# The low part of k in the second block's attention: one tile of two halves, or two zero-padded tiles

## The chip, the cores and the metric

The kernel runs on one core of one Trainium2 chip. The metric is the device time of one execution in microseconds (us). One launch computes two transformer blocks over 1,024 tokens of 1,024 features. The three runs shown below lie within 0.1% of each other.

## The reference, cut to what matters

The change lies in the second block's attention: 24 heads of 64 features in three groups of eight. In each group a query sees a causal window of its own residue class (dilation 1, 4 or 16), worked in blocks of 128 queries against the block itself and the one before it.

```python
HEAD_DIM = 64
HEADS_PER_GROUP = 8
DILATION_GROUPS = ((128, 1), (512, 4), (2048, 16))
...
    scores = jnp.einsum('bdhnqe,bdhnke->bdhnqk', qb.astype(jnp.float32),
                        kb.astype(jnp.float32)) * (e ** -0.5)
...
    scores = jnp.where(mask, scores, NEG_INF)
    m = jnp.max(scores, axis=-1)
    p = jnp.exp(scores - m[..., None])
    den = jnp.sum(p, axis=-1)
    o = jnp.einsum('bdhnqk,bdhnke->bdhnqe', p, vb.astype(jnp.float32)) / den[..., None]
```

## The kernel before, in words

**Precision.** TensorE multiplies in a reduced form of float32, so each operand is split into a hi and a lo part whose sum is exact; a product is hi·hi + hi·lo + lo·hi. Heads have only 64 features, so for the scores two of the three terms share one product over 128 partitions. `stack_q` makes, per head, a tile `qs` with hi on one half of the partitions and lo on the other; `stack_k` makes a tile `ks` with the hi part of k on both halves (the second half by a DMA of the first). The product of the two gives hi·hi + lo·hi. The third term, q's hi times k's lo, is a second product into the same place in PSUM; the lo parts of the two heads stand in the two halves of one tile `kl`, so this product contracts over 64 partitions, 0 to 63 for the first head of a pair and 64 to 127 for the second.

**Staging.** `block2` runs 12 pairs of heads (4 pairs hp in each of 3 groups g). A pair (`att_pair`) is: products q, k and v (`in2`, 48 matmuls of 512 columns each, whose weight tile is loaded as `w`, cast by ScalarE to `w2h` and subtracted by VectorE or GpSimd to `w2l`); rope; the stacks; transposes of v (`vt`); then for each head the scores (`as`: a `ks` and a `kl` product for each of 8 query blocks), the row maximum (`ap`, `amx`, VectorE), the exponentials (`ap`, ScalarE), transposes of those (`apt`), their split (`apth`, `aptl`) and the products with v (`ao`). Gate tiles (`z_conv`, `z_att`, `g_att`, `FILL`) follow each pair as filler for TensorE, and the taps of a convolution (`conv`) run on VectorE and GpSimd as background work. The masks, the exponentials and the sums are the same for every pair; a block has 256 key columns in the groups of dilation 1 and 4 (128 where it has no predecessor) and 128 in that of dilation 16.

**What sets the order.** The kernel records its instructions on virtual tiles, and a list scheduler in the kernel fixes one order per engine at build time: among the ready instructions it takes the one that is earliest in the program, up to 3,000 instructions ahead (`win`; 450 for SP, which issues the loads). Most tiles come from one pool of 50 pages of 128 x 1,024 float32 (`PAGES`). An instruction that writes a new tile takes a page when it is ordered, and it may do so early only if the count of live pages stays at 50 or under on the way to its own place in the program (`allowed`). On the chip it then waits until the page's last user is done.

Of the kernel before, what the change touches and what calls it, by code (L numbers as in the profile page):

```python
# [20 lines left out]
# ------------------------------------------------------------------ deferred program  # L21
# The kernel records its instructions on virtual tiles first; a list scheduler then fixes one
# order per engine (ready instructions by program order) and the instructions are issued to Tile
# in that order.
# [28 lines left out]
class VT:  # L53
    """A virtual tile: a slot of a pool from its first instruction to its last."""
# [13 lines left out]
class V:  # L68
    """A view of a virtual tile, resolved when its instruction is issued."""
# [24 lines left out]
    def region(self):  # L94
        """Bounds in the tile of what the view touches (at least)."""
        r = [(0, n) for n in self.t.shape]
        dims = list(range(len(r)))  # axes of the tile that the view still has
        if self.t.kind == "pb":  # a matmul that opens a group concerns its whole bank
            return tuple(r)
# [60 lines left out]
class Rec:  # L160
    """Records the calls on one engine."""
# [27 lines left out]
class Program:  # L189
    # margin of an operand that comes from another engine (us)  # L190
    LAT = 0.5

    def __init__(self, tc, nc, pools, limits):
        self.tc, self.nc, self.pools, self.limits = tc, nc, pools, limits
        self.engines = {"pe": nc.tensor, "act": nc.scalar, "dve": nc.vector, "pool": nc.gpsimd, "sp": nc.sync}
        self.ops, self.vts = [], []
        self.pe, self.act, self.dve, self.pool, self.sp = (Rec(self, e) for e in ("pe", "act", "dve", "pool", "sp"))
        self.count = 0
        self.bias = 0
        self.far = 0  # how far ahead of the oldest unfinished instruction one may be issued  # L200
        self.win = {None: 3000, "sp": 450}

    # -------------------------------------------------------------- tiles
# [6 lines left out]
    def dram(self, ap):  # L210
        """A DRAM scratch array whose order the program keeps."""
        return VT(self, "dram", ap.shape, F32, "dram", real=ap).v()

    # -------------------------------------------------------------- recording
    def record(self, eng, cost, lat, issue, reads, writes):
# [3 lines left out]
        op.dma = 0.0  # time that it takes of the DMA queues  # L219
# [25 lines left out]
    def price(self, eng, fn, a, kw, wr, rd):  # L245
        """Estimated time on the engine (us) and extra latency until the result can be used."""
# [35 lines left out]
    # -------------------------------------------------------------- scheduling  # L282
# [115 lines left out]
# ---------------------------------------------------------------- host layout  # L398
def _tiles(w, cols=None):
    """[K, C] -> [C/128, 128 (k within tile), K/128, 128 (c within tile)]."""  # L400
# [7 lines left out]
def _rows(w):  # L408
    """[K, C] -> [128 (k within tile), K/128, C]."""
# [5 lines left out]
def _vec(v):  # L415
    """[n*128] -> [128, n]."""
    return np.asarray(v).reshape(-1, P).T
# [10 lines left out]
def _selections():  # L428
    """Rows of the transposed trig tile: 16 cos, 8 cos, 16 sin, 8 sin, one."""
# [20 lines left out]
def _fourier_tables():  # L450
# [3 lines left out]
    tab = np.stack([np.cos(th) / 256, -np.sin(th) / 256])  # [2, 256 p, 1024 t = 4m+r]  # L454
    tab = tab.reshape(2, 2, P, 256, 4).transpose(1, 0, 2, 4, 3)  # [half, cs, p, r, m]
# [3 lines left out]
    ch = np.stack([np.concatenate([cc, cc], 1), np.concatenate([ss, ss], 1)], 1)  # [64, 2, 128]  # L459
# [3 lines left out]
def _band_masks():  # L463
    """Masks added to minus the scores: [prev | cur] band, [cur | none], and two causal blocks of 64."""
# [10 lines left out]
def prep(inp):  # L475
# [16 lines left out]
    o["wf"] = np.ascontiguousarray(g["w_fourier"][0].transpose(1, 0, 2))  # [64 c, 8 g, 64 e]  # L492
    o["ftab"], o["fch"] = _fourier_tables()
    o["w_out"] = _tiles(g["w_out"][0])
    o["memT"] = np.ascontiguousarray(g["mem"][0].T.reshape(2, 4, P, 256).transpose(0, 2, 1, 3))  # [2, p, 4 k, m]
# [3 lines left out]
    w = _tiles(g["w_mem_o"][0])  # [8 m, p, 8 k, 128]  # L499
# [30 lines left out]
# first 128-column tile of each part of w_in_2  # L530
# [3 lines left out]
# channel tiles of the convolution that run on ScalarE and GpSimd  # L534
POOL_CONV = (3,)
# steps of the latent attention with one of the memory's keys and values
MEM_AT = range(20,32)
# weight tiles of the experts split ahead of their products
AHEAD = 5
# and loaded ahead of them  # L540
RAW = 38
# of them before the first product
START = 38
# and right behind the first rows of an expert
# [3 lines left out]
# eighths of the work that VectorE and GpSimd can both do that GpSimd takes, by phase  # L548
# [3 lines left out]
# uses of the expert weights that are left when the second block's trig tables are loaded  # L552
TR = 16
# weight tiles of the second block that may be loaded before its input is there
# [3 lines left out]
# heads of the memory's attention by part of the output product  # L558
PARTS = ((0, 1), (2, 3))
# weight tiles of the experts loaded with each tile of these products  # L560
PRE = ((1, 1, 1, 1, 1, 1, 1, 1), (2, 2, 2, 2, 2, 2, 2, 2))
# instructions of the convolution behind each half product of the second block
TICKS = dict(zip("qkvgz", (1, 2, 1, 2, 2)))
# gate tiles behind each pair of heads, and tiles of the convolution ahead of each three pairs
# [4 lines left out]
class Halves:  # L569
    """Two tiles that hold one half each."""  # L570
# [8 lines left out]
class Kern(Program):  # L579
# [57 lines left out]
    # hi / lo halves of a float32 tile (exact: hi + lo == x)  # L637
    def split(self, x, base="sp", shape=(P, NT), hi="act", lo=None, scale=None, kind="pg"):
        """x: float32 AP in SBUF or PSUM; scale: per-partition column multiplied in."""
# [5 lines left out]
    def ve(self):  # L645
        """VectorE or GpSimd, by the share of the phase."""
# [18 lines left out]
    def wtile(self, dram, nk, base="w", hi="act", lo=None):  # L665
        """One stationary weight chunk [128, nk, 128] as hi / lo."""
# [9 lines left out]
    def gemm_t(self, w, xs, evac, n=NT, base="mm", ticks=2):  # L676
        """evac(c, ps): ps[128 cols, tokens c..] = sum_k w[:, k, :]^T xs[k], half of the tokens at a time."""
# [12 lines left out]
    def tick(self, last=None, n=2):  # L690
        """Background work (a vector queue, and one on ScalarE and GpSimd), a few instructions per half product."""
# [8 lines left out]
    def rsqrt(self, out, a, n):  # L700
        """out = a ** -0.5 on a small [128, n] tile (sqrt, reciprocal, one Newton step)."""
# [9 lines left out]
    def rsqrt_dve(self, out, a, n):  # L711
        """The same without a table of ScalarE: a guess from the exponent and three Newton steps."""
# [10 lines left out]
    def touch(self, func, after):  # L723
        """Have the table of an activation function in place once the instructions of after are done."""
# [4 lines left out]
    def colsum(self, tiles, n=8):  # L729
        """Sum over features (partitions of all tiles) -> psum [128 tok, n]: natural token layout."""  # L730
# [7 lines left out]
    def bcast_rows(self, col, evac, n=8):  # L738
        """[128 tok, n] small tile -> evac(tokens, psum): the token vector along the free axis in every partition."""
# [16 lines left out]
    # ------------------------------------------------------------------ trig  # L756
    def trig(self):
        """Transposed trig rows [49, 1024] for both position sets (block 1 freqs use positions, block 2 positions_2)."""
# [12 lines left out]
        # 2 pi = A + B + C with A, B of 12 bits; k = k1 + k0, k1 a multiple of 2048  # L771
# [48 lines left out]
    # ------------------------------------------------------------------ block 1, first half  # L820
    def block1_in(self):
# [3 lines left out]
        # the first weights and tokens come in halves, for an early start  # L825
# [20 lines left out]
        # latents: raw products (row factor deferred) times the gain, and their squares  # L846
# [34 lines left out]
        for name, n in (("q_lat", 3), ("kv_lat", 2)):  # L881
            # rx (rx^2 S / n + eps)^-1/2 = (S / n + eps / rx^2)^-1/2
# [7 lines left out]
        # rope key (rows 64..127, twice)  # L890
# [1137 lines left out]
```

## Time and profile before

| | before |
|---|---|
| device time, median of 3 runs | 2846.16 us (2844.48 to 2846.61) |
| the profiled execution, first to last instruction | 2844.7 us |
| TensorE busy | 2742.3 us, 96% of the span |
| VectorE busy | 2083.7 us, 73% |
| ScalarE busy | 1366.3 us, 48% |
| GpSimd busy | 479.1 us, 17% |
| mean granted TensorE clock | 0.970 of 2.4 GHz |
| second block's attention (first to last score product) | 1602.9 to 2482.1 us |

The profile is of one execution; its span is 1.5 us under the median of the timed runs. TensorE's matmuls are pipelined, so the "busy" time of one matmul is longer than its share of the engine: what a matmul costs is the distance from its start to the start of the next.

### The profile page before, as it was taken

To read this page: it belongs to the slowest core of one execution; us is meant where nothing else is said; L and a number is where in the kernel's file an instruction comes from. 1 tells how busy PE (TensorE), PEld (TensorE's weight loads), DVE (VectorE), ACT (ScalarE), POOL (GpSimd) and SP (SyncE) were. 2 spreads that over 40 slices of the span, in tenths; PEclk is the share of its full clock that TensorE was granted. 3 is DMA by queue.
4 is the path that set the end of the run, shared out by engine and by line. 5 is a ranking of instruction groups with operands and counts; after the bars stand their busy time and mean duration, and the time that the engine had idled before them with its cause. 6 is when DMAs were issued, how large, how long until landed. Compare 5 with 4: busy or idle time off the path is not lost. (4 is left out here: it accounts for less than half of the span.)

```text
span 2844.7 us, 35896 instructions
## 1 busy us (share of the span) xinstructions
PE 2742.3 (96%) x13230; PEld 2271.2 (80%) x13230; DVE 2083.7 (73%) x3075; ACT 1366.3 (48%) x2177; POOL 479.1 (17%) x246
## 2 busy tenths in 40 slices
PE   8999999999996999999979989999999999999998
PEld 6888898888874888888868777877888788887887
DVE  7368876358567899988968888787699886549553
ACT  6157766234345777777852445244233344423221
POOL 1124565111023200000010333201000002001000
PEclk9999999999997999999989998999999899999999
DMA  4000113345267999999942112112112133348941
GB/s 178 25 35 8 36 53 125 143 157 193 96 238 284 347 362 360 357 375 392 391 151 104 32 51 78 56 60 89 64 40 70 64 120 141 141 140 297 343 180 52
DMA packets 130143, 457.06 MB, mean 161 GB/s; under 512 B 15298, under 2 KB 17538, under 8 KB 129968
## 3 DMA queue, kind: packets, MB, share of 16 engines
q1 hardware_dynamic: 125360, 438.00, 41.9%
q0 software_dynamic: 4608, 16.78, 2.3%
q8 instruction: 104, 1.70, 0.2%
q14 instruction: 71, 0.58, 0.1%
HBM read 378.73 MB, written 69.70 MB: 158 GB/s over the span
## 5 line engine op out<-in xcount | busy, mean ns | idle before, releaser
L180 DVE SCALAR_TENSOR_TENSOR conv<-u,convw,conv 128x1023 f32<-128x1023 f32 (+21 forms) x210 | 290.1, 1387 | 2.3
L180 DVE TENSOR_TENSOR w_upl<-w_up,w_uph 128x1024 fp32r<-128x1024 f32 x128 | 149.2, 1220 | 22.5 <-ACT w_uph L180 22.0
L180 DVE TENSOR_TENSOR w_downl<-w_down,w_downh 128x1024 fp32r<-128x1024 f32 x128 | 148.9, 1219 | 13.3 <-ACT w_downh L180 12.7
L180 DVE TENSOR_TENSOR w_gatel<-w_gate,w_gateh 128x1024 fp32r<-128x1024 f32 x123 | 144.0, 1219 | 8.2 <-ACT w_gateh L180 5.7
L180 ACT CAST w_gateh<-w_gate 128x1024 fp32r<-128x1024 f32 x128 | 125.7, 1055 | 5.7 <-issue 3.4
L180 ACT CAST w_downh<-w_down 128x1024 fp32r<-128x1024 f32 x128 | 126.0, 1055 | 1.4 <-PE ea L180 1.4
L180 ACT CAST w2h<-w 128x1024 fp32r<-128x1024 f32 x80 | 83.2, 1048 | 90.5 <-DMA w<-in_w_in_dram 82.9
L180 ACT CAST w_uph<-w_up 128x1024 fp32r<-128x1024 f32 x128 | 125.8, 1055 | 1.4 <-PE ea L180 0.7
L180 POOL TENSOR_TENSOR w2l<-w,w2h 128x1024 fp32r<-128x1024 f32 x16 | 42.9, 2682 | 421.4 <-ACT w2h L180 389.6
L180 POOL TENSOR_TENSOR wl<-w,wh 128x1024 fp32r<-128x1024 f32 (+3 forms) x31 | 56.2, 1814 | 314.1 <-ACT wh L180 285.2
L180 POOL TENSOR_TENSOR conv<-conv,ct 128x1023 f32<-128x1023 f32 (+29 forms) x30 | 80.6, 2688 | 163.7 <-ACT ct L180 163.2
L180 DVE TENSOR_TENSOR w2l<-w,w2h 128x1024 fp32r<-128x1024 f32 x64 | 87.9, 1376 | 25.7 <-ACT w2h L180 25.1
L180 DVE CUSTOM_DVE_ANT_0 ap<-as,mask 128x128 f32<-128x128 f32 (+1 forms) x192 | 59.9, 352 | 62.0 <-PE as L180 56.8
L180 ACT CAST wh<-w 128x1024 fp32r<-128x1024 f32 (+3 forms) x71 | 62.5, 894 | 77.4 <-DMA w<-in_w_convout_dram 28.4
L180 ACT ACTIVATE ap<-ap,amx 128x128 f32<-128x128 f32 (+1 forms) x192 | 85.5, 447 | 26.7 <-DVE amx L180 26.3
L180 DVE TENSOR_TENSOR ptl<-pt,pth 128x512 fp32r<-128x512 f32 x128 | 81.4, 683 | 8.8 <-ACT pth L180 6.9
L180 ACT ACTIVATE p<-p,mx 128x1024 f32<-128x1024 f32 x64 | 73.8, 1155 | 23.5 <-DVE mx L180 17.2
L180 POOL TENSOR_SCALAR p<-p,sum 128x1024 f32<-128x1024 f32 x64 | 74.5, 1170 | 58.8 <-DVE sum L180 50.6
L180 PE MATMUL ea<-w_gatel,hth 128*128 128x512 f32 x256 | 80.1, 394 | 0.7 <-DVE w_gatel L180 0.7
L180 PE MATMUL eb<-w_uph,hth 128*128 128x512 f32 x256 | 80.5, 394 | 0.1
L180 PE MATMUL ea<-w_gateh,hth 128*128 128x512 f32 x256 | 80.6, 395 | 0.0
L180 PE MATMUL eb<-w_upl,hth 128*128 128x512 f32 x256 | 79.5, 392 | 0.7 <-DVE w_upl L180 0.5
(553 smaller groups left out, 8669.9 us busy)
## 6 DMA issues: line engine op xcount, KB each, us to landing
w_gate<-in_w_gate_dram SPq DMA_DIRECT2D x128, 512.0 KB
w_up<-in_w_up_dram SPq DMA_DIRECT2D x128, 512.0 KB
w_down<-in_w_down_dram SPq DMA_DIRECT2D x128, 512.0 KB
w<-in_w_in_dram SPq DMA_DIRECT2D x89, 512.0 KB
wada<-in_w_adaT_dram SPq DMA_DIRECT2D x24, 512.0 KB
convr<-cd SPq DMA_DIRECT2D x16, 512.0 KB
amd<-sg SPq DMA_DIRECT2D x16, 512.0 KB
ks<-ks SPq DMA_DIRECT2D x24, 256.0 KB
```

What stands on the lines that cost most here:

```text
L180: getattr(k.engines[eng], fn)(*[r(x) for x in a], **{n: r(x) for n, x in kw.items()})
```

## The change

`stack_k` makes two `kl` tiles per pair in place of one. Each holds the lo part of its own head on that head's 64 partitions, and zeros, written by a GpSimd memset, on the other 64. The second score product then takes all 128 partitions of `qs` and of `kl`; the zeros meet q's lo part. The count of products, of weight loads, of subtractions and of DMAs is the same; 24 memsets of 64 x 1,024 and 12 pages are new.

```diff
     def stack_k(self, o):
-        x, l = [self.page("ks", F32R) for _ in range(2)], self.page("kl", F32R)
+        x, l = ([self.page('ks', F32R) for _ in range(2)], [self.page('kl', F32R) for _ in range(2)])
         a, b = slice(0, 64), slice(64, P)
         for i, (own, far) in enumerate(((a, b), (b, a))):
+            self.pool.memset(l[i][far].bitcast(F32), 0.0)
             self.act.copy(x[i][own], o[own])
             self.sp.dma_start(x[i][far].bitcast(F32), x[i][own].bitcast(F32))
-            self.dve.tensor_tensor(l[own], o[own], x[i][own].bitcast(F32), OP.subtract)
+            self.dve.tensor_tensor(l[i][own], o[own], x[i][own].bitcast(F32), OP.subtract)
         return x, l
...
                     op = self.pe.matmul(sb, qs[h][:, q], kst[h][:, kk], start=True, stop=False)
...
-                    self.pe.matmul(sb, qs[h][r, q], kl[r, kk], start=False, stop=True)
+                    self.pe.matmul(sb, qs[h][:, q], kl[h][:, kk], start=False, stop=True)
```

The rest of the change removes comments. A memset depends on nothing but its page, so the scheduler orders it up to 3,000 instructions ahead of its place. GpSimd's order in the last experts of the first block (`hg` is the gather of an expert's rows, `x<-ey` the scatter-add of its result) was:

```order
L1392 DMA hg_11024<-hrow_84,idx 128x1024
L1401 DMA x_4_85<-ey_11107,idx 1024x1024
L1392 DMA hg_11353<-hrow_84,idx 128x1024
L1401 DMA x_4_85<-ey_11463,idx 1024x1024
L1392 DMA hg_11704<-hrow_84,idx 128x1024
```

and is now:

```order
L1392 DMA hg_11032<-hrow_84,idx 128x1024
L1401 DMA x_4_85<-ey_11115,idx 1024x1024
L1392 DMA hg_11361<-hrow_84,idx 128x1024
L1401 DMA x_4_85<-ey_11471,idx 1024x1024
L180 MEMSET kl_11537 64x1024
L180 MEMSET kl_11550 64x1024
L1392 DMA hg_11716<-hrow_84,idx 128x1024
```

Five pairs' memsets (ten pages) stand in this way between the experts' gathers and scatters, and a sixth pair's right behind the last scatter; before, no page of the attention was taken there.

On SP, which issues the loads, the weight tiles of the second pair stood ahead of the first pair's `ks` DMAs (`w` tiles 3234, 3243, 3255 and 3267 are the first gate tile and the second pair's q, k and v):

```order
L180 DMA w_3234_14040<-in_w_in_dram 128x1024
L180 DMA w_3243_14108<-in_w_in_dram 128x1024
L180 DMA w_3255_14194<-in_w_in_dram 128x1024
L180 DMA w_3267_14292<-in_w_in_dram 128x1024
L180 DMA ks_14316<-ks_14316 64x1024
L180 DMA ks_14325<-ks_14325 64x1024
```

Now two of the four (3256 and 3269, the k and v tiles) stand behind them:

```order
L180 DMA w_3235_14066<-in_w_in_dram 128x1024
L180 DMA w_3244_14134<-in_w_in_dram 128x1024
L180 DMA cd_104<-conv_13840 128x1024
L180 DMA ks_14344<-ks_14344 64x1024
L180 DMA ks_14352<-ks_14352 64x1024
L180 DMA w_3256_14462<-in_w_in_dram 128x1024
L180 DMA w_3269_14535<-in_w_in_dram 128x1024
```

The same holds for the `ks` DMAs of the second pair: four tiles ahead of them before, two now.

On TensorE the second pair's scores were followed by twelve gate matmuls before the first transpose of exponentials (`apt`):

```order
L180 MATMUL as_14911<-ks_14856,qs_14767 128x256
L180 MATMUL as_14911<-kl_14871,qs_14767 128x256
L180 MATMUL z_conv_14873<-h2l_13483,w2h_14684 128x512
L180 MATMUL z_conv_14873<-h2h_13471,w2l_14699 128x512
...
L180 MATMUL z_conv_14873<-h2h_13527,w2h_14684 128x512
L180 MATMUL apt_14944<-ident,ap_14926 128x128
```

Now the transpose follows at once:

```order
L180 MATMUL as_14914<-ks_14866,qs_14787 128x256
L180 MATMUL as_14914<-kl_10944,qs_14787 128x256
L180 MATMUL apt_14935<-ident,ap_14924 128x128
L180 MATMUL as_14937<-ks_14866,qs_14787 128x128
L180 MATMUL as_14937<-kl_10944,qs_14787 128x128
```

Between the first score product and the last `ao` of a pair stood 60, 53 and 41 filler matmuls in the first three pairs, and now stand 50, 30 and 31; in the fourth, fifth and seventh pair there are more than before (64, 49 and 66 became 72, 56 and 76).

## Rows read from the trace of the kernel before

**Rows 1.** The page, span and busy TensorE.

```profile
span 2844.7 us, 35896 instructions
PE 2742.3 (96%) x13230; PEld 2271.2 (80%) x13230; DVE 2083.7 (73%) x3075; ACT 1366.3 (48%) x2177; POOL 479.1 (17%) x246
```

**Rows 2.** Stretches of the attention: length, PE, PEld, DVE, ACT, POOL busy, granted clock, DMA.

```profile
1660.00:1735.00 75.00, 67.69 (x300) 54.07 (x299) 62.83 (x99) 34.47 (x70) 27.62 (x10) 0.91 0.15 50
...
2120.00:2195.00 75.00, 75.00 (x363) 61.12 (x362) 71.77 (x117) 30.16 (x73) 4.81 (x2) 1.00 0.19 64
...
sum 896.00, PE 878.64 PEld 711.06 DVE 695.13 ACT 356.61 POOL 120.98; mean PE 73.22 PEld 59.25 DVE 57.93 ACT 29.72 POOL 10.08
```

**Rows 3.** The score products by form (count, busy us, mean ns).

```profile
L180 PE MATMUL as<-ks,qs 128*128 128x256 f32 x96 | 37.1, 386 | 0.0
L180 PE MATMUL as<-ks,qs 128*128 128x128 f32 x96 | 32.1, 334 | 0.0
L180 PE MATMUL as<-kl,qs 64*128 64x256 f32 x96 | 37.7, 393 | 0.0
L180 PE MATMUL as<-kl,qs 64*128 64x128 f32 x96 | 33.7, 351 | 0.0
```

**Rows 4.** Timeline of TensorE, 256 columns (start us, us, instruction).

```profile
1855.02 0.39 PE L180 MATMUL as<-kl,qs 64*128 64x256 f32 x1
...
1855.65 0.38 PE L180 MATMUL as<-kl,qs 64*128 64x256 f32 x1
...
1857.55 0.39 PE L180 MATMUL z_conv<-h2h,w2l 128*128 128x512 f32 x1
1857.78 0.40 PE L180 MATMUL z_conv<-h2h,w2h 128*128 128x512 f32 x1
```

**Rows 5.** Timeline of TensorE, scores of 128 columns.

```profile
2241.13 0.33 PE L180 MATMUL as<-ks,qs 128*128 128x128 f32 x1
...
2243.17 0.33 PE L180 MATMUL as<-ks,qs 128*128 128x128 f32 x1
```

**Rows 6.** Timeline of TensorE, first block, 256 columns on 128 partitions.

```profile
686.10 0.28 PE L180 MATMUL ms<-mkh,mqh 128*128 128x256 f32 x1
...
688.14 0.28 PE L180 MATMUL ms<-mkh,mql 128*128 128x256 f32 x1
```

**Rows 7.** Timeline of TensorE, 128 columns on 128 partitions.

```profile
2268.05 0.56 PE L180 MATMUL ao<-apth,vt 128*128 128x128 f32 x4
2268.45 0.44 PE L180 MATMUL z_att<-h2h,w2h 128*128 128x512 f32 x1
```

**Rows 8.** Four slow-clock stretches of the attention, columns as in group 2.

```profile
1981.00:1987.80 6.80, 6.80 (x17) 5.15 (x18) 4.50 (x24) 3.82 (x17) 0.00 (x0) 0.50 0.23 88
...
2243.80:2250.60 6.80, 6.80 (x18) 5.10 (x18) 5.03 (x19) 3.17 (x16) 0.00 (x0) 0.50 0.00 0
2254.00:2264.30 10.30, 10.30 (x34) 8.55 (x35) 5.90 (x24) 4.92 (x20) 0.00 (x0) 0.50 0.00 1
...
2482.70:2489.50 6.80, 6.80 (x27) 5.91 (x26) 3.01 (x13) 3.70 (x13) 0.00 (x0) 0.50 0.42 157
```

**Rows 9.** Timeline of TensorE, idle time ahead of the transposes of v.

```profile
1602.13 1.11 PE L180 MATMUL vt<-ident,vf 128*128 128x128 f32 x4 [3.18 <-ACT vf L180]
...
1676.00 1.75 PE L180 MATMUL vt<-ident,vf 128*128 128x128 f32 x7 [7.31 <-ACT vf L180]
```

**Rows 10.** A GpSimd memset (groups), and taps on VectorE (timeline).

```profile
L180 POOL MEMSET bd<- 128x1024 f32 x1 | 0.9, 942 | 0.0
...
1656.51 1.26 DVE L180 SCALAR_TENSOR_TENSOR conv<-u,convw,conv 128x1019 f32<-128x1019 f32 x1
1662.37 3.31 DVE L180 SCALAR_TENSOR_TENSOR conv<-u,convw,conv 128x1018 f32<-128x1018 f32 x1
```

**Rows 11.** The split of the weight tiles in the attention (groups).

```profile
L180 DVE TENSOR_TENSOR w2l<-w,w2h 128x1024 fp32r<-128x1024 f32 x48 | 64.2, 1338 | 10.3 <-ACT w2h L180 10.1
L180 ACT CAST w2h<-w 128x1024 fp32r<-128x1024 f32 x60 | 62.8, 1049 | 79.7 <-DMA w<-in_w_in_dram 79.4
```

More of the change, by code (lines that the diff above doesn't have):

```diff
@@ L1686, in stack_k @@
     def stack_k(self, o):
-        x, l = [self.page("ks", F32R) for _ in range(2)], self.page("kl", F32R)
+        x, l = [self.page("ks", F32R) for _ in range(2)], [self.page("kl", F32R) for _ in range(2)]
         a, b = slice(0, 64), slice(64, P)
         for i, (own, far) in enumerate(((a, b), (b, a))):
+            self.pool.memset(l[i][far].bitcast(F32), 0.0)
             self.act.copy(x[i][own], o[own])
             self.sp.dma_start(x[i][far].bitcast(F32), x[i][own].bitcast(F32))
-            self.dve.tensor_tensor(l[own], o[own], x[i][own].bitcast(F32), OP.subtract)
+            self.dve.tensor_tensor(l[i][own], o[own], x[i][own].bitcast(F32), OP.subtract)
         return x, l
```

## Prediction

> **What bounds the kernel now.** I read the page first. TensorE is busy for 96% of 2844.7 us [rows 1], so the question is what a change does to TensorE's own time. The busy time by stretches says the same of the second block's attention: in 896 us it is busy for 878.6, and of the 17.4 us that are missing 14 lie in its first 216 us, the first three pairs of heads (one of the three stretches of this is shown, 7.3 us) [rows 2]. VectorE comes next. It is at 71.8 of 75 us in its fullest stretch and at 695 of 896 over the whole [rows 2], while ScalarE and GpSimd have more than half of their time to spare.
>
> Then the score products, by form: 96 of each of four kinds, 384 in all [rows 3]. Their mean durations (334 to 393 ns) say little, because matmuls overlap. The timeline gives the real price, the distance between starts. In a run of scores with 256 columns, two products (a `kl` and a `ks`) take 1855.65 - 1855.02 = 0.63 us [rows 4]. With 128 columns eight products lie between the starts 2241.13 and 2243.17, which is 0.255 us each or 0.51 for two [rows 5]. Half of the columns save only a fifth of the time, so most of the price does not depend on columns. Products that take all 128 partitions and load new weights each time show no such price: 17 starts of 256 columns lie between 686.10 and 688.14 in the first block, 0.12 us each [rows 6]; these add to one place of PSUM just as the scores do. Four of 128 columns take 2268.45 - 2268.05 = 0.40 us in the same attention, 0.10 each [rows 7]. Both kinds ran at the full clock, as the scores of rows 4 and 5 did. What the scores alone have is the alternation of a product over 128 partitions with one over 64; it costs about 0.19 us per product with 256 columns and 0.155 with 128, whichever of the two comes second.
>
> The clock comes last. TensorE has eleven stretches at half clock (1.2 GHz) in the attention. Those at the start follow idle time: TensorE waited 3.18 and 7.31 us for the copy of v ahead of its transposes [rows 9]. Four others, 30.7 us in all, have TensorE busy throughout [rows 8]; scores and transposes of exponentials stand in or just ahead of each, and the clock is granted at 0.50 although the engine never stops.
>
> **The change part by part.**
>
> *The products.* Their count stays. If every product takes all partitions, I price it by the nearest rows: 96 couples of 256 columns go from 0.63 to 0.24 us, 96 couples of 128 from 0.51 to 0.20. That is 96 x 0.39 = 37.4 and 96 x 0.31 = 29.8, together 67 us of TensorE time, 5.6 per pair. The bounds: nothing, if the price is not that of the alternation; 67 plus a few us where a transpose stood between two scores and paid as well.
>
> A page speaks against this. The Trainium skill, "TensorEngine Tiling", section Overview, promises up to twice the speed for a contraction of 64 or less, since two row tiles can work side by side; by that, padding gives away half of the array. The same page, section Key Properties, also says that changing the tiling mode drains the engine. Rows 4 and 5 agree with the drain and show nothing of the gain, since each half-array product stands between two full ones.
>
> *What of the 67 us reaches the end.* In pairs 4 to 12 (50 us of it) TensorE has almost no idle time, so its saving is the stage's, unless another engine takes over. VectorE is the one that can. Its fullest 75 us hold 71.8 us of work [rows 2], which does not fit into 75 - 5.6 = 69.4; a pair like that loses 2.4 of 5.6 us. The mean over the attention is 695/896 = 0.78, and less the 67 us it is 695/829 = 0.84, so most pairs fit. I take 85% of the 50, so 42 us. In the first three pairs (17 us) TensorE already waits for others; I take 60%, 10 us. Sum 52; bounds 25 (VectorE binds in every pair) and 67.
>
> *The clock.* The four busy stretches at half clock lose up to 30.7/2 = 15 us [rows 8]. With shorter drains the array works in a larger part of each of these stretches. The rows do not show whether that is enough to hold the clock, and a saving of scores inside these stretches is counted already. I take half, 8 us; bounds 0 and 15.
>
> *The memsets.* A GpSimd memset of 128 x 1,024 takes 0.94 us [rows 10]; 24 of half the partitions are at most 23 us on an engine that is idle for most of the span. Two things can make them dear. A VectorE tap of the convolution takes 1.26 us alone and 3.31 beside GpSimd's work [rows 10], so each of the 14 memsets that fall into the attention may lengthen a VectorE instruction; bounds 0 and 14 x 2 = 28 us of VectorE time, most of it hidden; I take 3. And a memset that waits for its page holds up what is behind it on GpSimd: gathers and scatters in the experts (each gather is one whole expert ahead of its use) and quarters of the weight splits in the attention. I take nothing for the gathers: ahead of them is the cover of 24 weight tiles' products, and without it each would cost its own wait.
>
> *The pages and the order.* This is the cost that I expect. Ten of the 50 pages are taken during the last experts, and the loads, which take pages as well, come later: behind both of the first two pairs' `ks` DMAs stand two weight tiles that stood ahead of them. Inside the experts I see no harm, since the order has pages to spare there. In the first three pairs 10 + 23 + 10 = 43 filler matmuls move out from among the scores and exponentials. A filler takes 1857.78 - 1857.55 = 0.23 us [rows 4], so 43 x 0.23 = 10 us of cover is lost where TensorE then waits for VectorE and ScalarE. The start of the block, where the fourth weight tile now waits for a page that is released late, I put at another 5 us, about one tile's way: landing, cast 1.05 us, subtraction 1.34 us [rows 11], and the wait for the page. Sum 15 us lost; the lower bound is 5 (the waits of rows 9 were there anyway), the upper 45 (nine tiles' way at 5 us).
>
> The weight loads onto TensorE's array, the subtractions that make `kl`, the copies and the DMAs stay as they are, in count and size; they cost nothing new, since the same work did fit before.
>
> *The sum.* 52 + 8 - 3 - 15 = 42 us less. Against the profiled span, 2844.7 - 42 = 2802.7; the timed median lies 1.5 us over that span, so 2804 us.
>
> **The rivals.**
>
> *The pages decide, and it gets slower.* If loads come so late that TensorE waits for weights in many pairs, each such tile costs about 5 us (as above). For it: ScalarE already waits 79.4 us for weight DMAs in the attention [rows 11]; TensorE itself waits for none of them there. Against it: the fillers are back, and more of them, from the fourth pair on. The gain of 57 us is gone at 57/5, about 12 tiles; 20 tiles give 2846 + 100 - 57 = 2889 us. I give 8% to a result slower than before by this way, most of it near 2860.
>
> *VectorE takes the place of TensorE.* The softmax of each pair is a chain VectorE, ScalarE, TensorE, and VectorE has the convolution to do as well. If only 25 of the 52 us reach the end and the order still costs 15, with 3 for the memsets and nothing from the clock, then 2846 - 25 + 18 = 2839; with 5 of the clock 2834. For it: 71.8 of 75 us in one stretch; against it: 0.78 on the mean. 17%.
>
> *Everything comes through.* 67 + 15 of the clock, less 5 for the order and nothing for the memsets: 2846 - 77 = 2769. For it: the order's new waits may lie where TensorE waited before. 13%.
>
> *The alternation is not what costs.* If the second score product is dear for another reason (its operands, or adding to PSUM right behind the first), padding changes nothing, and the order's 15 us remain: 2861. Against it: rows 6, which add to PSUM at 0.12 us, and the `ks` products, which are as dear as the `kl` ones when they follow one. 2%. A variant is the skill's side-by-side rule: were the 64-partition products at half price today, the padded ones would cost 192 x 0.05 = 10 us more, so 2871; rows 4 and 5 leave no room for it, and its chance is within these 2%.
>
> **How the numbers follow.** My forecast, 60%: 2804 us, between 2785 and 2825. Through the rivals the range is 2766 to 2842: it leaves out the slower tail (10%) and a little at the fast end. A change within 0.2% (5.7 us) is about what a measurement of this kernel can tell from none. Faster by more than that has my forecast, the full gain and nearly all of the VectorE case: 60 + 13 + 14 = 87%. Within it 3%, slower 10%.
>
> **What would show it.** In the profile after: all 384 score products as 128-partition forms, starts about 0.12 us apart with 256 columns and 0.10 to 0.11 with 128 where nothing stands between; the attention from first to last score some 45 us shorter. The clock at 1.00 in stretches that answer to rows 8. The order's cost as TensorE idle time in the first three pairs and at the block's start, beyond the 14 us of now, with weight tiles or the softmax as its releasers. VectorE's share of the attention at 0.82 or more. Wrong would be: starts still 0.25 to 0.31 us apart; TensorE idle for over 60 us in the attention; or experts that take longer, if ten pages fewer hold up their weights.

## The result and the profile after

| | median us (runs) | ratio to before, 95% interval |
|---|---|---|
| before | 2845.32 (2842.32 to 2846.61, 4 runs) | |
| after | 2770.22 (2767.57 to 2771.41, 4 runs) | 0.9737 [0.9723, 0.975] |

75 us are gone, 33 more than the forecast of 42. The time lies in the range, near its fast end, and at the place of the rival "everything comes through" (2769).

The page of the kernel after, span and busy time of each engine:

```profile
span 2769.3 us, 36068 instructions
PE 2659.9 (96%) x13230; PEld 2232.0 (81%) x13230; DVE 2096.2 (76%) x3075; ACT 1362.1 (49%) x2177; POOL 505.6 (18%) x270
```

TensorE has as many instructions as in [rows 1], its share of the span is still 96%, and its busy time fell by 82 us. GpSimd has the 24 memsets more (246 instructions before).

**Where the time went.** Take the attention from the first transpose of v to the first matmul of `g_conv` behind it, all twelve pairs and the fillers between them. This is its row in the stretches of before (columns as in group 2), whole, then pairs 1 to 3, then pairs 4 to 12:

```profile
1598.40:2520.40 922.00, 904.64 (x4159) 732.94 (x4157) 695.25 (x1166) 363.69 (x778) 118.84 (x44) 0.96 0.23 82
...
1598.40:1853.50 255.10, 241.11 (x1062) 194.09 (x1061) 196.69 (x297) 111.06 (x213) 78.97 (x30) 0.92 0.18 60
1853.50:2520.40 666.90, 663.53 (x3099) 538.86 (x3097) 498.55 (x870) 252.63 (x565) 39.87 (x14) 0.97 0.25 90
```

The same three stretches after, then two of 75 us: the one that answers to the first of [rows 2], and the one in which VectorE is fullest:

```profile
1601.40:2446.10 844.70, 821.38 (x4154) 692.67 (x4152) 709.60 (x1167) 359.50 (x779) 129.33 (x56) 0.98 0.26 90
...
1601.40:1838.20 236.80, 218.47 (x1056) 182.28 (x1055) 212.38 (x296) 108.78 (x212) 81.70 (x36) 0.96 0.21 67
1838.20:2446.10 607.90, 602.91 (x3100) 510.40 (x3098) 497.22 (x871) 250.72 (x567) 47.63 (x20) 0.99 0.29 99
...
1646.00:1721.00 75.00, 64.65 (x312) 54.12 (x311) 70.00 (x97) 33.62 (x68) 27.12 (x12) 0.93 0.17 57
2159.00:2234.00 75.00, 74.02 (x366) 61.52 (x365) 74.47 (x112) 27.45 (x62) 2.55 (x1) 1.00 0.27 91
```

The stage is 77.3 us shorter, 18.3 of it in pairs 1 to 3 and 59.0 in pairs 4 to 12; all else in the span is 1.9 us longer (2844.7 - 922.0 = 1922.7 before, 2769.3 - 844.7 = 1924.6 after). The experts, in which ten pages are now held, lost nothing that shows. Length less PE gives TensorE's idle time: 17.4 us before, 23.3 after. In pairs 4 to 12 it is 5.0 of 607.9, so TensorE still sets the end there.

**The products.** The score products by form, after: all 384 contract over 128 partitions.

```profile
L180 PE MATMUL as<-ks,qs x192: 220/286/562, 1606.3 to 2411.0; 128*128 128x256 f32 x96, 128*128 128x128 f32 x96
L180 PE MATMUL as<-kl,qs x192: 272/281/416, 1606.5 to 2411.1; 128*128 128x256 f32 x96, 128*128 128x128 f32 x96
```

The timeline of TensorE, after, in two runs of scores that nothing interrupts (start, us, instruction):

```profile
1839.17 0.28 PE L180 MATMUL as<-kl,qs 128*128 128x256 f32 x1
...
1839.88 0.28 PE L180 MATMUL as<-kl,qs 128*128 128x256 f32 x1
...
2196.23 0.27 PE L180 MATMUL as<-kl,qs 128*128 128x128 f32 x1
...
2197.79 0.27 PE L180 MATMUL as<-kl,qs 128*128 128x128 f32 x1
```

With 256 columns six steps from start to start take 0.71 us, 0.118 each (0.315 in [rows 4]); with 128 columns fourteen take 1.56 us, 0.111 each (0.255 in [rows 5]).

**The clock.** The three pairs in which the stretches of [rows 8] lie, before, each from the first transpose of v on:

```profile
1976.80:1994.00 17.20, 17.20 (x69) 13.03 (x70) 11.13 (x40) 7.79 (x29) 0.00 (x0) 0.80 0.34 114
2238.90:2271.10 32.20, 32.20 (x133) 25.70 (x134) 21.90 (x58) 14.35 (x47) 0.00 (x0) 0.73 0.10 29
2471.80:2489.00 17.20, 17.20 (x75) 13.87 (x76) 8.39 (x38) 10.38 (x41) 0.00 (x0) 0.72 0.34 124
```

The same three pairs after, from the same transpose on:

```profile
1949.10:1966.30 17.20, 17.20 (x119) 15.38 (x118) 13.18 (x50) 13.29 (x46) 0.00 (x0) 1.00 0.23 68
2194.50:2226.70 32.20, 32.11 (x181) 27.14 (x182) 32.04 (x69) 16.58 (x51) 0.00 (x0) 1.00 0.29 95
2404.70:2421.90 17.20, 17.20 (x115) 15.23 (x115) 13.10 (x46) 15.18 (x48) 0.00 (x0) 1.00 0.45 157
```

TensorE is busy throughout in both (but for 0.1 us), and the granted clock went from between 0.72 and 0.80 up to 1.00. By the higher clock and the cheaper scores together, 36% to 72% more products fit into the same time (the first row: 69 to 119). In the whole stage, the stretches at half clock add up to 81.9 us before (eleven) and to 27.3 after; these are the four that are left:

```profile
1624.40:1631.20 6.80, 5.80 (x22) 4.93 (x21) 5.25 (x10) 6.18 (x14) 0.97 (x2) 0.50 0.00 0
1668.80:1679.00 10.20, 7.09 (x31) 6.70 (x32) 8.08 (x25) 7.97 (x19) 0.00 (x0) 0.50 0.22 51
1740.50:1743.90 3.40, 3.40 (x14) 3.01 (x14) 3.37 (x2) 1.55 (x3) 2.96 (x2) 0.50 0.44 104
2334.40:2341.20 6.80, 6.80 (x22) 5.64 (x22) 6.80 (x16) 2.27 (x4) 0.00 (x0) 0.50 0.00 0
```

The second of them holds the wait for the copy of v that stood in [rows 9], only 0.1 us shorter than before:

```profile
1671.11 1.76 PE L180 MATMUL vt<-ident,vf 128*128 128x128 f32 x7 [7.21 <-ACT vf L180]
```

The last of the four has TensorE busy throughout, but it begins 1.4 us after a wait of 1.48 us for GpSimd (first line). What half clock costs is read from it too, in TensorE's timeline:

```profile
2333.01 2.13 PE L180 MATMUL cs<-ones,csq 128*128 128x1 f32 x15 [1.48 <-POOL csq L180]
...
2337.18 0.63 PE L180 MATMUL g_att<-h2h,w2l 128*128 128x512 f32 x1
...
2339.74 0.63 PE L180 MATMUL g_att<-h2h,w2l 128*128 128x512 f32 x1
```

Six steps from start to start take 2.56 us, 0.427 each, where a filler of this form takes 0.23 at full clock [rows 4]. So about half of such a stretch is lost, and by this estimate (81.9 - 27.3) / 2 = 27 us came back through the clock. The mean granted clock of the whole span (0.970 before, 0.979 after) gives the same: 0.030 x 2844.7 - 0.021 x 2769.3 = 27 us.

**VectorE.** The longest waits of VectorE in the stage, after (us in total, times, longest):

```profile
DVE rt L180 <- PE q L180: 19.4, 10, 5.0
DVE ap L180 <- PE as L180: 14.4, 18, 1.8
```

Before, it waited for the scores most of all:

```profile
DVE ap L180 <- PE as L180: 56.8, 38, 5.7
DVE rt L180 <- PE q L180: 36.5, 16, 5.9
```

Its share of the stage rose from 695.3/922.0 = 0.75 to 709.6/844.7 = 0.84, as forecast. It made up for that by waiting less for TensorE. In its fullest 75 us (from 2159.0, above) it is busy for 74.5, so there it has nothing left to give; TensorE is busy for 74.0 of the same 75.

### The profile page after: what moved, and what is told of

The parts are those of the page before. It is cut to its first block, busy times and chain, and to the rows that moved or that the text cites. A ratio compares the mean times of both kernels' runs of the same rounds, so it can differ in the third digit from the quotient of the medians.

```text
span 2769.3 us, 36068 instructions
## 1 busy us (share of the span) xinstructions
PE 2659.9 (96%) x13230; PEld 2232.0 (81%) x13230; DVE 2096.2 (76%) x3075; ACT 1362.1 (49%) x2177; POOL 505.6 (18%) x270
## 5 line engine op out<-in xcount | busy, mean ns | idle before, releaser
L180 DVE SCALAR_TENSOR_TENSOR conv<-u,convw,conv 128x1003 f32<-128x1003 f32 (+19 forms) x210 | 298.0, 1426 | 2.2
L180 POOL TENSOR_TENSOR conv<-conv,ct 128x1023 f32<-128x1023 f32 (+29 forms) x30 | 74.8, 2493 | 115.5 <-ACT ct L180 115.1
L1401 POOL DMA_INDIRECT x<-ey,idx x16 | 25.4, 1586 | 302.4 <-ACT ey L180 193.7
```

The costliest lines, as they stand in the source:

```text
L180: getattr(k.engines[eng], fn)(*[r(x) for x in a], **{n: r(x) for n, x in kw.items()})
L1401: self.nc.gpsimd.indirect_dma_start(out=rows.ap(), out_offset=bass.IndirectOffsetOnAxis(ap=idx.ap(), axis=0), in_=x.ap(), in_offset=None, ...
```

## The experiments

The theory: a change between products over 128 and over 64 partitions costs TensorE time, each time it happens, and padding takes 384 such changes away. The first rival: the time came from the new order, pages and loads, and not from the products. The second: a product over 64 partitions is dear in itself. A third question is why the clock gave back more than the busy stretches of [rows 8] hold.

### The order alone

All of the new kernel's tiles, memsets and order; only the second product contracts over its head's 64 partitions again. Each engine's order is that of after.

```
-self.pe.matmul(sb, qs[h][:, q], kl[h][:, kk], start=False, stop=True)
+self.pe.matmul(sb, qs[h][r, q], kl[h][r, kk], start=False, stop=True)
```

> Tiles, memsets and order of the changed kernel, but the second score product contracts over 64 partitions again. If the alternation of 128 and 64 partitions is what the change took away, and its early pages only cost, the time is that of the kernel before plus the cost of the order: by the prediction's term 2845 + 15 = 2860 us (bounds 2850 to 2890); by the idle time that the changed kernel's trace shows in the attention (about 8 us more than before) 2853. If the new order itself brings part of the gain, it is under 2840.

Measured: 2856.57 us (2855.43 to 2863.15, 5 runs; before on the same chip 2844.82), ratio 1.004 [1.0026, 1.0055]. Its stage, pairs 1 to 3 and pairs 4 to 12:

```profile
1600.10:2537.00 936.90, 916.91 (x4154) 740.92 (x4152) 711.96 (x1167) 362.37 (x779) 127.31 (x56) 0.94 0.23 81
...
1600.10:1863.30 263.20, 247.78 (x1055) 198.34 (x1054) 211.53 (x296) 109.53 (x212) 81.70 (x36) 0.89 0.18 60
1863.30:2537.00 673.70, 669.13 (x3100) 542.58 (x3098) 500.43 (x871) 252.84 (x567) 45.61 (x20) 0.96 0.25 90
```

The order and the memsets by themselves lose 12 us, so the first rival falls: the gain is that of the products, and with the order held fixed it is 2856.57 - 2770.22 = 86 us. The loss isn't where I looked for it. TensorE idles 20.0 us in place of 17.4; what grew is the half clock, from 81.9 us to 109.2 (41.0 to 58.0 of it in pairs 1 to 3). The profiled run was the slowest of the five, 6.6 us over their median. Over all five the mean granted clock is 0.968, against 0.970 before, and by that the clock makes up only some 6 to 7 of the 12 us, an estimate (0.032 x 2856 less 0.030 x 2843).

### The memset behind its own k

After, but each memset waits for the rope of its own pair's k, so that no page is taken early. The order is then nearly that of before: leaving tile numbers aside, on TensorE 136 of 13,073 matmuls stand elsewhere (442 in after), on SP 4 of 900 DMAs (14 in after).

```
-self.pool.memset(l[i][far].bitcast(F32), 0.0)
+self.pool.memset(l[i][far].bitcast(F32), 0.0).deps.add(len(self.ops) - 2)
```

> The changed kernel, but each memset has to wait for the rope of its own k, so that no page of the attention is taken in the experts and the loads stand where they stood before the change. If early pages cost something, this is the changed kernel less that cost: 2755 us by the prediction's term of 15 us, 2762 by the 8 us of extra idle time. If the order costs nothing, it is 2770.

Measured: 2764.05 us (2761.33 to 2766.88, 4 runs; before 2844.82), ratio 0.9716 [0.97, 0.9732]. Its stage:

```profile
1597.00:2437.30 840.30, 820.66 (x4160) 693.46 (x4158) 704.20 (x1165) 358.61 (x777) 137.74 (x66) 0.98 0.26 89
```

6 us below after by the medians, but the two intervals overlap at 0.9723 to 0.9732, so this pair doesn't settle what the order is worth without the changes. TensorE idles 19.6 us here and 23.3 in after.

### The old tiles, with the products grouped

Before, with its one `kl` tile and its products over 64 partitions, but all first products of a score tile come ahead of all second ones, so that far fewer changes happen. Nothing is padded.

```
-op = self.pe.matmul(sb, qs[h][:, q], kst[h][:, kk], start=True, stop=False)
+op = self.pe.matmul(sb, qs[h][:, q], kst[h][:, kk], start=i % half == 0, stop=False)
...
-self.pe.matmul(sb, qs[h][r, q], kl[r, kk], start=False, stop=True)
+low.append((sb, qs[h][r, q], kl[r, kk], i % half == half - 1))
...
+for sb, lq, lk, last in low:
+    self.pe.matmul(sb, lq, lk, start=False, stop=last)
```

> The kernel before, with 64 partitions in the second product, but all first products of a tile of scores stand ahead of all its second ones, so that TensorE goes from 128 to 64 partitions and back once per tile (and where a transpose comes in between) and not at every product. If each change between 128 and 64 partitions costs its 0.15 to 0.19 us, most of the gain comes without any padding: 2845 less 0.7 x 75 = 2790 us. If a product over 64 partitions is dear by itself, only the first products get cheaper: 2845 - 37 = 2808 us, and second products still start 0.25 to 0.31 us apart when they follow one another.

Measured: 2783.19 us (2781.4 to 2785.69, 4 runs; before 2844.82), ratio 0.9779 [0.9763, 0.9795]. Its stage:

```profile
1596.40:2459.90 863.50, 843.78 (x4159) 702.33 (x4157) 699.81 (x1166) 361.40 (x778) 113.88 (x44) 0.98 0.25 87
```

Half of the array stays unused in 192 products, and still 62 of the 75 us are there. In TensorE's order 116 changes are left of 384. This is the plainest evidence that the change of size costs, not the size.

### One head of two

After, but only the first head of each pair uses the whole padded tile.

```
-self.pe.matmul(sb, qs[h][:, q], kl[h][:, kk], start=False, stop=True)
+s = slice(0, P) if h == 0 else r
+self.pe.matmul(sb, qs[h][s, q], kl[h][s, kk], start=False, stop=True)
```

> The changed kernel with the padded product for the first head of each pair alone; the second head's second product takes 64 partitions. Half of the alternations are left. If each of them has a price of its own, the time is midway between e1_order_alone and the changed kernel: about 2812 us. If a part of the gain is the clock's, and the clock holds only when the scores are dense throughout, it is nearer to e1_order_alone: 2825 or more.

Measured: 2817.38 us (2813.3 to 2819.61, 4 runs; before 2844.82), ratio 0.9904 [0.9887, 0.992]. Its stage:

```profile
1599.80:2486.60 886.80, 865.56 (x4154) 715.57 (x4152) 709.34 (x1167) 360.74 (x779) 128.36 (x56) 0.97 0.25 86
```

With half of the changes (192) it lies between the order alone (2856.57) and after (2770.22), 39 of 86 us down the way.

### Both products over 64 partitions

Before, with the first product over its head's 64 partitions as well. It leaves out the product of q's lo part with k's hi part.

```
-op = self.pe.matmul(sb, qs[h][:, q], kst[h][:, kk], start=True, stop=False)
+op = self.pe.matmul(sb, qs[h][r, q], kst[h][r, kk], start=True, stop=False)
```

> The kernel before with both score products over the 64 partitions of their own head; this leaves out the product of q's low part with k's high part. No score alternates with another any more; what is left are the changes against transposes, fillers and products with v. If the alternation costs, this is near the grouped kernel (2783 us): 2775 to 2790, scores starting 0.12 (256 columns) and 0.10 to 0.11 us (128) apart when they follow one another. If a product over 64 partitions is dear by itself, now all 384 are: 2845 us or more, starts 0.25 to 0.31 us apart. If fewer partitions also cost the clock, more of the attention is at half clock than in the grouped kernel (41 us).

Measured: 2813.16 us (2810.61 to 2814.0, 4 runs; before on the same chip 2844.41), ratio 0.9889 [0.9874, 0.9904]. Its timeline of TensorE:

```profile
1845.06 0.28 PE L180 MATMUL as<-kl,qs 64*128 64x256 f32 x1
...
1845.77 0.28 PE L180 MATMUL as<-kl,qs 64*128 64x256 f32 x1
1845.98 0.50 PE L180 MATMUL z_conv<-h2h,w2l 128*128 128x512 f32 x1
...
1848.43 0.39 PE L180 MATMUL as<-ks,qs 64*128 64x256 f32 x1
1848.75 0.44 PE L180 MATMUL apt<-ident,ap 128*128 128x128 f32 x2
```

Six steps between 64-partition products in a row take 0.71 us, 0.118 each, the same as 128-partition ones in after. At the end of the run the next product, over 128 partitions, comes 0.21 later, and a score that stands alone between transposes holds the engine for 0.32. So the second rival falls too. I had expected 2775 to 2790 and missed: I had counted the changes inside the couples only. Scores stand among transposes and other products over 128 partitions, and 256 changes are left, more than in the grouped kernel. The stage:

```profile
1603.10:2489.00 885.90, 872.66 (x4154) 714.15 (x4153) 693.56 (x1163) 356.56 (x773) 112.13 (x44) 0.97 0.24 84
```

### Two tiles, zeroed once

The memset behind its own k, but with two padded tiles for all pairs, zeroed once: 2 memsets in place of 24. TensorE, VectorE, ScalarE and SP then have the order of before row for row, and GpSimd has the two memsets more; so against before this is the padding by itself.

```
-x, l = [self.page("ks", F32R) for _ in range(2)], [self.page("kl", F32R) for _ in range(2)]
+x, l = [self.page("ks", F32R) for _ in range(2)], self.kls[self.turn_k % len(self.kls)]
+self.turn_k += 1
...
-    self.pool.memset(l[i][far].bitcast(F32), 0.0)
...
+self.turn_k, self.kls = 0, [[self.page("kl", F32R) for _ in range(2)] for _ in range(1)]
+for s in self.kls:
+    for i, far in enumerate((slice(64, P), slice(0, 64))):
+        self.pool.memset(s[i][far].bitcast(F32), 0.0).deps.add(len(self.ops) - 2)
```

> As e2_late_memset, but the two padded tiles are fixed: zeroed once ahead of the first pair, and only their low parts rewritten, so 2 memsets in place of 24. If the memsets cost VectorE the 3 us that the prediction put on them, 2761 us; if they cost nothing, 2764; above 2767 if holding two pages throughout costs more than the memsets did.

Measured: 2760.38 us (2757.92 to 2761.25, 5 runs; before 2844.41), ratio 0.9706 [0.9692, 0.9719]. This is the fastest kernel that computes everything, below after by about 10 us, with intervals that don't touch. The padding alone is thus worth 84 us, and what the change brought with it, early pages, order and memsets together, costs 10 of them. Its stage:

```profile
1596.70:2433.60 836.90, 816.21 (x4160) 688.83 (x4158) 695.13 (x1167) 360.95 (x778) 118.29 (x44) 0.99 0.26 90
```

Against before the stage is 85.1 us shorter in one order: TensorE's busy time is 88.4 us less and its idle time (20.7) 3.3 more. VectorE's busy time is that of before (695.1 against 695.3; after 709.6, with 12 memsets inside the stage). Against the kernel with the late memsets, 3.7 us are gained in the medians, with intervals that overlap.

### No second product

The memset behind its own k, without the second product; its operands are still made. It leaves out the product of k's lo part.

```
-op = self.pe.matmul(sb, qs[h][:, q], kst[h][:, kk], start=True, stop=False)
+op = self.pe.matmul(sb, qs[h][:, q], kst[h][:, kk], start=True, stop=True)
...
-self.pe.matmul(sb, qs[h][:, q], kl[h][:, kk], start=False, stop=True)
```

> As e2_late_memset, but the second score product is left out (its operands are still made). It measures what the 192 padded products cost now: 96 x 0.12 + 96 x 0.10 = 21 us, so 2743 us, if TensorE still sets the stage's end; 2755 or more if VectorE or the softmax chain does by now.

Measured: 2741.72 us (2738.16 to 2743.82, 4 runs; before 2844.41), ratio 0.964 [0.9624, 0.9656]. Its stage:

```profile
1595.80:2415.20 819.40, 797.75 (x3968) 667.99 (x3966) 692.04 (x1166) 356.38 (x777) 133.62 (x65) 0.99 0.26 92
```

192 products less are 22 us less of the kernel, 0.12 each, which is what one costs in the timeline of after. So TensorE still sets the end: VectorE takes nothing of a further saving of this size.

### All together

The changes are counted in TensorE's order; stage and idle time are from the rows above (length, and length less PE); half clock is the sum of the stage's stretches with a grant of 0.50 in the trace. The last column is PE less half of the half clock, an estimate of TensorE's work as if at full clock.

| kernel | changes | stage us | idle us | half clock us | work at full clock us |
|---|---|---|---|---|---|
| the order alone | 384 | 936.9 | 20.0 | 109.2 | 862.3 |
| before | 384 | 922.0 | 17.4 | 81.9 | 863.7 |
| both over 64 | 256 | 885.9 | 13.2 | 59.6 | 842.9 |
| one head | 192 | 886.8 | 21.2 | 61.4 | 834.9 |
| grouped | 116 | 863.5 | 19.7 | 41.0 | 823.3 |
| after | 0 | 844.7 | 23.3 | 27.3 | 807.7 |
| late memsets | 0 | 840.3 | 19.6 | 30.7 | 805.3 |
| zeroed once | 0 | 836.9 | 20.7 | 17.1 | 807.7 |

The last column is close to a straight line. From before to after it falls by 56.0 us over 384 changes, 0.146 us each; by that rate the three kernels between should stand at 845.0, 835.7 and 824.6, and stand at 842.9, 834.9 and 823.3. The half clock falls with the changes too, from 82 to 109 us to 17 to 31, though idle time doesn't.

## Why the prediction came out as it did

The direction, the place and the mechanism were right; the likeliest case was too slow. Put beside the terms of the sum, from the rows of before and after:

| term | forecast us | measured us |
|---|---|---|
| what reaches the end of the products | -52 | -56.0 (work at full clock) |
| clock | -8 | -27.3 |
| cover in the first three pairs | +10 | +5.9 (idle time of the stage) |
| block start | +5 | +1.9 (span outside the stage) |
| memsets | +3 | not apart in this pair of kernels |
| sum | -42 | -75.5 (spans: -75.4) |

- **The clock is the step that failed**, with 19 of the 33 us. I counted only the four stretches of [rows 8] as those in which TensorE never stops, and gave back half of their loss. All four have no counterpart after. The seven others I left alone, since those at the start followed idle time [rows 9]; but together they fell as well, from 81.9 - 30.7 = 51.2 us to 27.3, though the wait of 7.2 us for the copy of v is still there. And the rows were read wrongly: nine of the eleven have TensorE busy throughout, 58 us in all. Three of those that I left out:

```profile
1762.50:1769.30 6.80, 6.80 (x29) 6.04 (x28) 4.19 (x15) 4.37 (x13) 2.78 (x1) 0.50 0.11 39
...
1994.60:1998.00 3.40, 3.40 (x16) 3.11 (x16) 2.29 (x3) 2.64 (x10) 0.00 (x0) 0.50 0.00 0
...
2472.50:2475.90 3.40, 3.40 (x11) 2.47 (x10) 2.37 (x14) 3.38 (x16) 0.00 (x0) 0.50 0.45 137
```

  The bound of 15 us was too tight: by the busy stretches alone it is 58/2 = 29 us, and half of all half clock in the stage is 41 us.
- **The products**: their price was too high and the discount on it too large; that the two nearly cancel was luck. I priced a change at 67/384 = 0.174 us, from runs of scores alone; the mean over all places is 0.146. Part of the difference shows in the timelines, of before and then of after:

```profile
1924.11 0.36 PE L180 MATMUL as<-ks,qs 128*128 128x256 f32 x1
1924.40 0.38 PE L180 MATMUL as<-kl,qs 64*128 64x256 f32 x1
1924.72 0.44 PE L180 MATMUL apt<-ident,ap 128*128 128x128 f32 x2
...
1855.09 0.36 PE L180 MATMUL as<-ks,qs 128*128 128x256 f32 x1
1855.29 0.28 PE L180 MATMUL as<-kl,qs 128*128 128x256 f32 x1
```

  Where the `ks` follows a transpose, as in these rows, the step from `ks` to `kl` goes from 0.29 to 0.20 us, which saves 0.09; in a run of scores it saves 0.19. In TensorE's order of before 75 of the 192 `ks` products don't follow a `kl`. The step out of a `kl` is as dear to a transpose (0.32) as to a score (0.31). Of the 56 us, everything reached the end. The 15% that I took off for VectorE and the 40% in the first pairs weren't lost: VectorE's share of the stage is 0.84 and its fullest 75 us are now full (74.5, where [rows 2] have 71.8), but over the stage it took the rest from its waits for scores (56.8 to 14.4 us). The run without the second product, which lost another 22 us, says the same. I compared VectorE's work with the shorter stage, and not its waits with what TensorE gives back.
- **The order**: the cost exists, but not as I wrote it. With the changes kept it is 12 us, close to my 15, and in the profiled run, the slowest of five, it comes nearly all as half clock (109.2 against 81.9 us), not as idle time; over all five runs the clock is some 6 to 7 of the 12. With the changes gone, TensorE's idle time in the stage is 5.9 us more, 4.3 of it in the first three pairs (18.3 against 14.0); 3.3 of the 5.9 are there with the order of before too (the kernel with two tiles), so the order's own part is smaller still. Order and memsets together are the 10 us between after and that kernel. The 1.9 us outside the stage are not evidence of a cost at the block's start: the three kernels with the old or nearly old order and one `kl` tile lie at 1920.3 to 1926.3 there, wider than that.
- **The memsets**: I expected that each may lengthen a VectorE instruction as GpSimd's other work does [rows 10]. It doesn't. In after, this tap has a memset beside it and takes as long as alone:

```profile
1853.83 1.26 DVE L180 SCALAR_TENSOR_TENSOR conv<-u,convw,conv 128x1004 f32<-128x1004 f32 x1
...
1854.08 0.95 POOL L180 MEMSET kl<- 64x1024 f32 x1 [8.03 <-PE ao L180]
```

  Six taps in the stage of after overlap a memset and no other work of GpSimd, and none takes more than 1.28 us; the 30 that overlap GpSimd's two-operand instructions and no memset take 2.1 us on the mean (before, 25 taps and 2.0 us). VectorE's busy time in the stage did rise by 14.4 us, and is back where it was with two memsets and the order of before. But without the second product, where the stage has 22 memsets, it is 692.0 us, less than before. So the rise is not that of the memsets. Likely it is that of the order, which puts more of GpSimd's two-operand work beside VectorE's taps (the three kernels with the order of after lie at 709.3 to 712.0 us); this isn't shown singly. Between the kernels with late memsets and with two of them lie 3.7 us by the medians, which is near the 3, but within the uncertainty; their orders differ a little, and no cause is shown.
- **The rivals**: "the pages decide" didn't happen; TensorE's idle time is 23 us, not the 60 that I named. "VectorE takes the place" didn't either. "The alternation is not what costs" is refuted by the grouped kernel. "Everything comes through" was right in its time (2769) and half right in its reason: less of the products (56, not 67) and more of the clock (27, not 15). I gave it 13% where the table of half clock over the whole stage would have asked for more.

A page's rule stands beside this. The Trainium skill, "TensorEngine Tiling", section Key Properties, says that a change of the tiling mode drains the engine. The runs agree in that each change costs time, 0.146 us on the mean. The Trainium skill, "TensorE: Matmul & The Clock Gate", section Why this matters for your kernels, says that a single product with a contraction of 32 takes as long as one of 128. For 64 the run with both products over 64 partitions agrees, where they follow one another (0.118 us, as in after). The gain from two row tiles side by side was not tried: no run here lets the two heads' products overlap.

**What stays open.** Why the clock is granted less where changes are many is not shown. The table shows that the two go together in eight kernels. Idle time sorts the stretches further. In the four kernels with 0 or 116 changes every stretch at half clock holds a wait of TensorE of 0.3 us or more, or begins less than 3 us after one. In the four with 192 changes or more, 27 to 48 us of half clock (before: 30.7) begin more than 9 us after any such wait. So the half clock that begins away from waits is gone at 116 changes already, and what is left lies at waits. Whether the rest came from the changes themselves, or from what stands around them, no run tells apart.

## What to carry to other kernels

Before a product over part of the partitions is made cheaper or dearer, count how often TensorE's order goes from one contraction size to another: here each change cost 0.146 us of work, and with each went about 0.07 us of clock on the mean ((81.9 - 27.3) / 2 / 384), and padding with zeros or grouping by size takes it away. Look at the distance between starts, not at durations, and take half of the half clock of the whole stage as the bound of what a denser TensorE can get back. An engine whose share would rise to 0.84 need not bind, if its longest wait is for the engine that gets faster; and padding that is never overwritten is zeroed once, not per use.

## What the runs showed of the hardware that was not expected

- The granted clock falls to 0.50 while TensorE is busy without a gap: with the order alone it stays there from 1990.4 to 2010.9 us, with no wait of 0.3 us or more in the 234 us before. Half clock grows with the changes of contraction size in the order: 17 to 31 us without changes, 41 with 116, 60 and 61 with 256 and 192, 82 and 109 with 384.
- Half of the partitions save GpSimd no time in a memset. The group of the new memsets, after, 64 x 1,024 each (the one of 128 x 1,024 in [rows 10] took 942 ns):

```profile
L180 POOL MEMSET kl<- 64x1024 f32 x24 | 22.8, 950 | 281.7 <-PE as L180 53.9 <-DVE w2l L180 49.7 <-PE glu_b L180 49.6
```

- A memset on GpSimd doesn't lengthen VectorE's taps of the convolution: 1.26 us beside one (the rows above), as alone, against 3.31 beside other work of GpSimd [rows 10]. VectorE's work in the stage is 709.6 us with 12 memsets in it, 704.2 and 692.0 with 22, and 693.6 to 699.8 in the four kernels with none.
